# Two-layer diffusion trunk: most adaLN modulations computed on TensorE, and the first feed-forward begun on half of its scale

## The chip, the cores and the metric

The kernel runs on one core of a Trainium2 chip, as one program with one launch. The core has five engines that run side by side, each through its own list of instructions in order: TensorE (PE in the profile; its weight loads are PEld), VectorE (DVE), ScalarE (ACT), GpSimd (POOL) and SyncE (SP), which here starts nearly all the DMAs. The metric is the device time of an execution in microseconds (us).

## The reference, cut to what matters

The program is one step of a two-layer trunk over 128 context and 256 latent tokens of width 1024, in float32. All of a layer that matters here is this:

```python
mod = einsum('bd,de->be', silu(cond), w_ada) + b_ada     # w_ada 1024 x 9216, cond: c_ctx or c
mod = mod.reshape(batch, 9, 1, 1024)
h = rms_norm(x, norm_g[0]) * (1.0 + mod[:, 1]) + mod[:, 0]
x = x + 0.5 * mod[:, 2] * swiglu(h, w_gate[0], w_up[0], w_down[0])     # FFN_DIM = 2816
h = rms_norm(x, norm_g[1]) * (1.0 + mod[:, 4]) + mod[:, 3]
x = x + mod[:, 5] * mix(h)                                             # four mixers
h = rms_norm(x, norm_g[2]) * (1.0 + mod[:, 7]) + mod[:, 6]
x = x + 0.5 * mod[:, 8] * swiglu(h, w_gate[1], w_up[1], w_down[1])

def swiglu(h, w_gate, w_up, w_down):
    return (silu(h @ w_gate) * (h @ w_up)) @ w_down
```

The nine modulations of a layer are two vectors (one for each stream, `c_ctx` and `c`) times a matrix of 1024 x 9216 floats: 37.7 MB a layer, with little arithmetic. They depend on no token, so they may be computed at any time before the place that needs them.

## The kernel before, in words

The residual is kept feature-major, `xT` of [128, 8, 384]: 8 blocks of 128 features, 384 tokens. A product with a weight matrix keeps float32 accuracy by splitting: `split_unit` (lines 164 to 174) makes of a block of weights a rounded part `whi` on ScalarE (L169) and a rest `wlo` on VectorE (L173, sometimes GpSimd); `mm3` (L184 to 188) issues three matmuls per block of 128 x 128 weights: high by high, high by low, low by high. A matmul of 384 tokens is the unit of work on TensorE.

The order is: start (input, first norm), feed-forward (0,0), mixers of layer 0, feed-forward (0,1), feed-forward (1,0), mixers of layer 1, feed-forward (1,1). A feed-forward first makes 22 pairs of gate and up products (tiles `pg` and `pu`, 1056 matmuls), then the down products (`pd`, 528 matmuls). Right behind a norm, the first few products (`hidden`, L194) use the scaled but not yet normed residual `xs`, and the factor 1/rms and the shift come behind the product; two columns beside the 384 tokens carry the shift.

The modulations come in quarters of 256 columns, 72 in all. Five of the first eight are on TensorE (`ada_rows`, L238): the two conditionings are the stationary operand of 128 x 2, the quarter of `w_ada` is streamed, in float32. The other 67 quarters are done by `ada` (L257) without TensorE: VectorE multiplies and adds for one stream (L268, L271), ScalarE multiplies (L269, L274) and GpSimd adds (L275) for the other; VectorE then transposes and sums (L278, L279), and four small matmuls a batch put the result in place (L285). 28 quarters stand beside feed-forward (0,0), 20 beside (0,1), 16 beside (1,0), none beside (1,1): the hook in `ffn_body` issues the next quarter at a lower priority, and a scheduler at build time, which has a cost model of its own, fixes the order of each engine's list.

`start` (L372) takes the order of its parts from a string: the norm's statistics, three quarters of the shift through VectorE, and four quarters of the scale and one of the shift on TensorE. Only when all eight are done does the first feed-forward begin, since the two shift columns are part of its first products. SP has one queue, in order: an issue that waits for a free buffer holds up those behind it.

## Time and profile before

| | |
|---|---|
| Time, median of 3 runs | 2245.91 us (2243.18 to 2248.57) |
| Profiled execution, first to last instruction | 2244.0 us |
| PE busy | 2076.3 us, 93% |
| DVE busy | 1724.6 us, 77% |
| ACT, POOL busy | 1039.3 us, 942.2 us |
| HBM traffic over the span | 143 GB/s |

The profiled execution has no time of its own on the page beside its span; the median of the runs lies 1.9 us above that span, and this is taken as what lies around it. A matmul's busy time in the rows overlaps with the next one's, so rates are read from stretches of known work. Line numbers are those of the kernel before.

### The profile page before, as it was taken

The page shows a single profiled execution, that of the slowest core. Times are in us where ns is not written, and L with a number is a line of the kernel's source. Part 1 is how long each engine was busy: PE and PEld are TensorE (multiplying, and loading weights), DVE is VectorE, ACT ScalarE, POOL GpSimd, SP SyncE. Part 2 cuts the span into 40 slices and gives each one's busy share as a digit, 9 for nine tenths or more (in the row PEclk, how much of TensorE's full clock was granted, in tenths as well). Part 3 has the DMA queues.
Part 4 walks back from the last instruction along what each step waited for, and adds up shares of the span by engine and source line. Part 5 has one row for each costly group of instructions (what it writes and reads, how often), then busy time and mean ns, then how long its engine had stood idle before and what let it go on. Part 6 is the DMA issues. An engine that isn't in the chain of part 4 may idle for free. (4 is left out here: it accounts for less than half of the span.)

```text
span 2244.0 us, 33102 instructions
## 1 busy us (share of the span) xinstructions
PE 2076.3 (93%) x12150; PEld 1992.7 (89%) x12150; DVE 1724.6 (77%) x3198; ACT 1039.3 (46%) x1978; POOL 942.2 (42%) x855
## 2 busy tenths in 40 slices
PE   6988888999789997998998999999987999999999
PEld 3988788999679997998887999998976899999999
DVE  8999998778995469999899974467999745764433
ACT  5666554634234235765556643354333332463322
POOL 5556666433655237366476520134354531500000
PEclk8999999999889999999999999999998999999999
DMA  9466655444333244566555644344442321444342
GB/s 306 152 217 199 202 198 164 129 136 105 83 81 103 60 164 155 169 210 214 186 193 155 206 135 133 128 146 137 119 95 83 109 76 59 160 134 129 115 139 76
DMA packets 316515, 323.08 MB, mean 144 GB/s; under 512 B 42112, under 2 KB 287296, under 8 KB 315840
## 3 DMA queue, kind: packets, MB, share of 16 engines
q1 hardware_dynamic: 316080, 320.70, 46.1%
q8 instruction: 95, 1.56, 0.3%
q14 instruction: 68, 0.56, 0.1%
q10 hardware_dynamic: 272, 0.26, 0.0%
HBM read 313.25 MB, written 7.69 MB: 143 GB/s over the span
## 5 line engine op out<-in xcount | busy, mean ns | idle before, releaser
L169 ACT CAST whi<-raw 128x1024 fp32r<-128x1024 f32 x422 | 440.2, 1045 | 511.1 <-PE mg L187 133.3
L173 DVE TENSOR_TENSOR wlo<-raw,whi 128x1024 fp32r<-128x1024 f32 x324 | 434.8, 1343 | 226.9 <-ACT whi L169 223.8
L275 POOL TENSOR_TENSOR acc<-acc,acct 128x256 f32<-128x256 f32 x469 | 440.5, 939 | 334.7 <-ACT acct L274 306.4
L173 POOL TENSOR_TENSOR wlo<-raw,whi 128x1024 fp32r<-128x1024 f32 x98 | 244.9, 2505 | 289.9 <-ACT whi L169 244.2
L271 DVE SCALAR_TENSOR_TENSOR acc<-araw,cond,acc 128x256 f32<-128x256 f32 x469 | 323.5, 690 | 6.3
L274 ACT ACTIVATE acct<-araw,cond 128x256 f32<-128x256 f32 x469 | 214.1, 501 | 139.7 <-DVE accr L278 83.4
L188 PE MATMUL pd<-hh,wlo 128*128 128x384 f32 x704 | 240.8, 345 | 20.2 <-DVE wlo L173 20.2
L186 PE MATMUL pd<-hh,whi 128*128 128x384 f32 x704 | 240.5, 342 | 9.0 <-ACT whi L169 4.5
L187 PE MATMUL pd<-hl,whi 128*128 128x384 f32 x704 | 239.9, 341 | 0.0
L188 PE MATMUL pg<-hhi,wlo 128*128 128x384 f32 x544 | 184.8, 340 | 19.2 <-DVE wlo L173 19.0
L188 PE MATMUL pu<-hhi,wlo 128*128 128x384 f32 x544 | 184.7, 340 | 13.4 <-DVE wlo L173 13.1
L186 PE MATMUL pg<-hhi,whi 128*128 128x384 f32 x544 | 182.1, 335 | 0.4 <-ACT whi L169 0.4
L187 PE MATMUL pu<-hlo,whi 128*128 128x384 f32 x544 | 182.2, 335 | 0.0
L186 PE MATMUL pu<-hhi,whi 128*128 128x384 f32 x544 | 182.2, 335 | 0.0
L187 PE MATMUL pg<-hlo,whi 128*128 128x384 f32 x544 | 182.1, 335 | 0.0
L186 PE MATMUL mg<-hhi,whi 128*128 128x384 f32 x512 | 177.7, 347 | 0.0
L187 PE MATMUL mg<-hlo,whi 128*128 128x384 f32 x512 | 175.4, 343 | 0.0
L188 PE MATMUL mg<-hhi,wlo 128*128 128x384 f32 x512 | 174.5, 343 | 0.5 <-DVE wlo L173 0.5
L321 POOL TENSOR_SCALAR xg<-xT,gs 128x128 f32<-128x128 f32 (+1 forms) x96 | 101.9, 1074 | 150.9 <-DVE xT L432 150.8
L188 PEld LDWEIGHTS pd<-hh,wlo 128*128 128x128 f32 x704 | 134.0, 191 | 27.6 <-DVE wlo L173 27.6
L186 PEld LDWEIGHTS pd<-hh,whi 128*128 128x128 f32 x704 | 134.4, 191 | 11.3 <-ACT whi L169 5.4
L187 PEld LDWEIGHTS pd<-hl,whi 128*128 128x128 f32 x704 | 134.5, 191 | 0.1
(410 smaller groups left out, 4961.5 us busy)
## 6 DMA issues: line engine op xcount, KB each, us to landing
araw<-in_w_ada SPq DMA_DIRECT2D x67, 1024.0 KB
raw<-in_w_in SPq DMA_DIRECT2D x62, 1024.0 KB
raw<-in_ffn_w_gate SPq DMA_DIRECT2D x44, 1024.0 KB
raw<-in_ffn_w_up SPq DMA_DIRECT2D x44, 1024.0 KB
raw<-in_ffn_w_down SPq DMA_DIRECT2D x40, 1024.0 KB
raw<-in_w_branch SPq DMA_DIRECT2D x16, 512.0 KB
raw<-in_w_out SPq DMA_DIRECT2D x8, 1024.0 KB
raw<-in_w_ada SPq DMA_DIRECT2D x5, 1024.0 KB
```

The costliest lines, as they stand in the source:

```text
L169: nc.scalar.copy(hi, src)
L173: (eng or nc.vector).tensor_tensor(lo, src, hi.bitcast(F32), op=ALU.subtract)
L186: nc.tensor.matmul(ps, w[0], x[0], start=start, stop=False)
L187: nc.tensor.matmul(ps, w[0], x[1], start=False, stop=False)
L188: nc.tensor.matmul(ps, w[1], x[0], start=False, stop=stop)
L271: nc.vector.scalar_tensor_tensor(acc[0], raw[:, kk], self.cond[:, kk:kk + 1], acc[0], op0=ALU.mult, op1=ALU.add)
L274: nc.scalar.mul(t, raw[:, kk], self.cond[:, 8 + kk:9 + kk])
L275: self.last_add = nc.gpsimd.tensor_tensor(acc[1], acc[1], t, op=ALU.add)
L321: self.nc.gpsimd.tensor_scalar(xg[kk][:, a:e], self.xT[:, kk, a:e], gs[:, s, kk:kk + 1], None, op0=ALU.mult)
```

## The change

Of the 72 quarters, 54 go through TensorE as 27 halves of 512 columns, and 18 remain on VectorE, ScalarE and GpSimd. For a half, the two conditionings stand in 32 columns, the rest zeros (`cond32`), and the 8 blocks of `w_ada` go round the four groups of 32 columns of the array (`tile_position=(0, 32 * g)`), so that each group makes a part sum on its own 32 partitions of one PSUM tile: two blocks for each group, 8 matmuls with 512 float32 columns. `issue_after` chains the eight behind each other and behind the last product issued before. ScalarE copies the tile, four transposes turn it, and one VectorE reduction adds the four groups. In the feed-forwards two halves share one PSUM tile (the second writes its own columns of it), one copy and four transposes. There are 9, 6, 6 and 2 such halves in feed-forwards (0,0), (0,1), (1,0) and (1,1), one after every pair of units or so; the 18 quarters stand beside the down products of the first three, six each.

`start` now loads a half of the scale, then the first gate and up weights, then the other half, and begins six units (144 matmuls: gate and up of the first 256 columns, gate of the next) with the first half of the features as soon as that half of the scale is there; the shift comes later. Since the shift is not there yet, its effect on these six units is computed apart, as the same kind of grouped product of the raw weights with the shift (`pair_rows_times`, three times 8 matmuls of 256 columns), and added as a bias. The constants that the start loads shrink from 642 to 162 columns.

```diff
+        cond32 = self.const.tile([128, KD, 34], F32, name="cond32")
+        nc.vector.memset(cond32, 0.0)
+        nc.vector.tensor_copy(cond32[:, :, 2:4], self.cond.rearrange("p (s k) -> p k s", s=2))
+        self.cond32 = [cond32[:, :, 2 - 2 * i:34 - 2 * i] for i in range(2)]
...
+    def ada_load(self, l, mod, hf):
+        c0 = mod * D + 512 * hf
+        raws = []
+        for i in range(2):
+            raws.append(self.ap.tile([128, 4, 512], F32, tag="araw", name="araw", bufs=self.n_araw))
+            self.last_load = self.nc.sync.dma_start(raws[i], self.I["w_ada"][l, 512 * i:512 * i + 512, c0:c0 + 512].rearrange(
+                "(k p) n -> p k n", p=128))
+        return raws
+    def group_rows(self, ps, cols, blocks, first=True, last=True, behind=None):
+        for i, (kk, blk) in enumerate(blocks):
+            g = kk % 4
+            with self.after(behind):
+                behind = self.nc.tensor.matmul(ps[32 * g:32 * g + 32], cols[:, kk], blk, start=(i < 4 and first),
+                                               stop=(i >= 4 and last), tile_position=(0, 32 * g))
+    def group_cols(self, ps, n, e, out):
+        nc = self.nc
+        row = self.ring.tmp([128, n], "mrow")
+        nc.scalar.copy(row, ps)
+        tp = self.mxps([128, n // 128, 128], "acol")
+        for q in range(n // 128):
+            nc.tensor.transpose(tp[:, q], row[:, 128 * q:128 * q + 128], self.k(K_ID))
+        nc.vector.tensor_reduce(out, tp.rearrange("p q (g e) -> p e q g", g=4)[:, 0:e], axis=AX, op=ALU.add)
+    def pair_rows_times(self, cols, blocks, n, out):
+        ps = self.mxps([128, n], "arow")
+        self.group_rows(ps, cols, list(enumerate(blocks)))
+        self.group_cols(ps, n, 2, out)
+    def ada_half(self, l, mod, hf, raws):
+        t = self.small.tile([128, 2, 4], F32, tag="asum", name="asum")
+        self.pair_rows_times(self.cond32[0], [r[:, g] for r in raws for g in range(4)], 512, t)
+        c = slice(8 * mod + 4 * hf, 8 * mod + 4 * hf + 4)
+        self.nc.vector.tensor_tensor(self.mods[l][:, :, c], t,
+                                     self.prm[l][:, R_B:R_B + 72][:, c].unsqueeze(1).to_broadcast([128, 2, 4]), op=ALU.add)
+    def ada(self, *halves):
+        raws = self.ada_load(*halves[0])
+        for i, h in enumerate(halves):
             yield
-    def ada(self, l, mod, n=4):
-        """The same beside the tensor engine, n quarters from a modulation on, one at a time."""
-        nc = self.nc
-        ap = self.ap
-        xa = ap.tile([128, 2, 8 * n], F32, tag="xa", name="xa", bufs=1)
+            if i % 2 == 0:
+                ps, n = self.mxps([128, 512], "arow"), min(2, len(halves) - i)
+            r = i % 2
+            self.group_rows(ps, self.cond32[r], [(4 * h + g, raws[h][:, g]) for h in (1, 0) for g in range(4)],
+                            r == 0, r == n - 1, self.last_mm)
+            if r == n - 1:
+                t = self.small.tile([128, 4, 4], F32, tag="asum", name="asum")
+                self.group_cols(ps, 512, 2 * n, t[:, 0:2 * n])
+                for q, (l, mod, hf) in enumerate(halves[i - r:i + 1]):
+                    c = slice(8 * mod + 4 * hf, 8 * mod + 4 * hf + 4)
+                    self.nc.vector.tensor_tensor(
+                        self.mods[l][:, :, c], t[:, 2 * q:2 * q + 2],
+                        self.prm[l][:, R_B:R_B + 72][:, c].unsqueeze(1).to_broadcast([128, 2, 4]), op=ALU.add)
+            if i + 1 < len(halves):
+                raws = self.ada_load(*halves[i + 1])
...
-        next(shift)
+        wg, wu = I["ffn_w_gate"][0, 0], I["ffn_w_up"][0, 0]
+        def cols(w, c0):
+            t = self.ring.tile([128, KD, 256], F32, name="raw0")
+            nc.sync.dma_start(t, w[:, c0:c0 + 256].rearrange("(k p) n -> p k n", p=128))
+            return t
+        scale = [self.ada_load(0, 1, 0)]
+        raw = [cols(wg, 0), cols(wu, 0)]
+        scale.append(self.ada_load(0, 1, 1))
+        raw.append(self.wcols(wg, 256))
+        shift = [self.ada_load(0, 0, hf) for hf in range(2)]
+        self.up1 = self.wcols(wu, 256)
+        sh32 = self.ring.tile([128, KD, 32], F32, name="sh32")
+        nc.gpsimd.memset(sh32, 0.0)
+        units = [(0, 0), (1, 0), (0, 1), (1, 1), (2, 0), (2, 1)]
+        w, ps = {}, {}
+        def split(u):
+            r, m = u
+            w[u] = self.split_unit(raw[r][:, :, 128 * m:128 * m + 128], [128, KD, 128])
+            ps[u] = (self.mmps if r < 2 else lambda name: self.mxps([128, T], name))(name="pg" if r != 1 else "pu")
+        def rows(u, k0, k1):
+            for k in range(k0, k1):
+                self.mm3(ps[u], (w[u][0][:, k], w[u][1][:, k]), [t[:, k, 0:T] for t in self.xs], k == 0, k == KD - 1)
+        for hf in range(2):
+            self.ada_half(0, 1, hf, scale[hf])
+            self.scales(0, 0, self.nx[2], 4 * hf, 4 * hf + 4)
+            for k in range(4 * hf, 4 * hf + 4):
+                self.early_part(k, True)
+            if hf == 0:
+                for u in units[:3]:
+                    split(u)
+                    rows(u, 0, 4)
+        for u in units[:3]:
+            rows(u, 4, KD)
+        self.rstd()
+        for u in units[3:]:
+            split(u)
+            rows(u, 0, KD)
+        for hf in range(2):
+            self.ada_half(0, 0, hf, shift[hf])
         self.early_shift()
-        with self.after(self.last_add):
-            for k in range(KD):
-                self.norm_scale(k)
+        nc.vector.tensor_copy(sh32[:, :, 0:2], self.mods[0][:, :, 0:8].rearrange("p s k -> p k s"))
+        bias = []
+        for r in range(3):
+            bias.append(self.small.tile([128, 2, 2], F32, tag="sb", name="sb", bufs=3))
+            self.pair_rows_times(sh32, [raw[r][:, kk] for kk in range(KD)], 256, bias[r])
+        self.ready = [(ps[u], bias[u[0]][:, :, u[1]]) for u in units]
+        for k in range(KD):
+            self.norm_scale(k)
         self.norm()
...
+    def ffn_body(self, l, i, jobs, beside, nxt):
         nc, I = self.nc, self.I
         g = None
 
         def hook(n):
-            with self.tc.high_priority(offset=-100):
-                for _ in range(n):
-                    next(jobs, None)
+            for _ in range(n):
+                next(jobs, None)
+        hook(1)
         hh, hl = [], []
         for j in range(KF // 2):
-            rg = self.wcols(I["ffn_w_gate"][l, i], 256 * j)
-            ru = self.wcols(I["ffn_w_up"][l, i], 256 * j)
+            begun = 2 - j if (l, i) == (0, 0) and j < 2 else 0
+            rg = None if begun else self.wcols(I["ffn_w_gate"][l, i], 256 * j)
+            ru = None if begun == 2 else self.up1 if begun else self.wcols(I["ffn_w_up"][l, i], 256 * j)
             for m in range(2):
                 f = 2 * j + m
-                wg = self.split_unit(rg[:, :, 128 * m:128 * m + 128], [128, KD, 128])
-                wu = self.split_unit(ru[:, :, 128 * m:128 * m + 128], [128, KD, 128])
-                pg = self.hidden(wg, "pg")
-                pu = self.hidden(wu, "pu")
+                wg = None if begun else self.split_unit(rg[:, :, 128 * m:128 * m + 128], [128, KD, 128])
+                wu = None if begun == 2 else self.split_unit(ru[:, :, 128 * m:128 * m + 128], [128, KD, 128])
+                pg = self.shifted(*self.ready.pop(0)) if begun else self.hidden(wg, "pg")
+                pu = self.shifted(*self.ready.pop(0)) if begun == 2 else self.hidden(wu, "pu")
                 sg = self.wp.tile([128, T], F32, tag="nt", name="sg", bufs=2)
                 nc.scalar.activation(out=sg, in_=pg, func=AF.Silu)
                 nc.vector.tensor_tensor(sg, sg, pu, op=ALU.mult)
@@ -466,12 +558,11 @@
                 hl.append(self.ring.tile([128, T], F32R, name="hl"))
                 nc.scalar.copy(hh[f], sg)
                 nc.vector.tensor_tensor(hl[f], sg, hh[f].bitcast(F32), op=ALU.subtract)
-            hook(2)
+            hook(1)
         if nxt is None:
             self.nx = None
         else:
             self.norm_begin(*nxt)
-            self.scales(*nxt, self.nx[2])
         g = self.gates(l, 2 * i, 0.5)
         cuts = {(0, 3): (0, 4), (1, 1): (4, 6), (1, 3): (6, 8)}
         for dg in range(2):
...
                         units = []
                 hook(1)
+                if f % 8 == 0:
+                    with self.tc.high_priority(offset=-100):
+                        next(beside, None)
+            if nxt is not None and dg == 0:
+                self.scales(*nxt, self.nx[2])
             for d in range(4):
                 self.down(units, acc[d], d, hh, hl)
                 self.resid(g, 4 * dg + d, acc[d])
                 if nxt is None and (dg, d) in cuts:
                     self.store(*cuts[dg, d])
-        for _ in jobs:
+        for _ in chain(jobs, beside):
...
             self.setup()
+            self.n_araw = 4
             with self.pool("ap") as self.ap:
                 self.start()
+            self.n_araw = 3
             for l in range(2):
                 if l:
                     self.norm()
                 else:
                     with self.after(self.last_load):
                         self.nc.sync.dma_start(self.cst[:, NC1:], self.I["cst2"])
-                self.ffn(l, 0, self.ada(l, 5, 16) if l else chain(self.ada(l, 2, 12), self.ada(l, 5, 16)), (l, 1))
+                halves = {(0, 0): (4, 13), (0, 1): (16, 22), (1, 0): (25, 31), (1, 1): (34, 36)}
+                quarters = {(0, 0): ((0, 6, 2, 2), (0, 7, 0, 4)), (0, 1): ((1, 2, 0, 4), (1, 3, 0, 2)),
+                            (1, 0): ((1, 6, 2, 2), (1, 7, 0, 4)), (1, 1): ()}
+                jobs = [self.ada(*((h // 18, h // 2 % 9, h % 2) for h in range(*halves[l, i]))) for i in range(2)]
+                beside = [chain(*(self.ada_beside(*q) for q in quarters[l, i])) for i in range(2)]
+                self.ffn(l, 0, jobs[0], beside[0], (l, 1))
                 self.norm()
                 self.mixers(l)
                 self.norm()
-                self.ffn(l, 1, iter(()) if l else self.ada(1, 0, 20), None if l else (1, 0))
+                self.ffn(l, 1, jobs[1], beside[1], None if l else (1, 0))
```

The lists of the engines show what this moves. In the rows, the line numbers behind L are those of each kernel's own text (`mm3` is L186 to L188 before, L185 to L187 now). First PE at the start, before: `xr` is the input, `arow` a modulation's row, `mx` from `sqacc` and `nr` the norm, and the last row the first product.

```order
L234 MATMUL mx<-cst,xr 128x128 x24
L246 MATMUL arow<-raw,cond 2x256 x8
L363 MATMUL mx<-cst,sqacc 128x1 x3
L246 MATMUL arow<-raw,cond 2x256 x16
L368 MATMUL mx<-cst,nr 128x128 x3
L251 MATMUL mx<-cst,mrow 128x2 x6
L246 MATMUL arow<-raw,cond 2x256 x16
L251 MATMUL mx<-cst,mrow 128x2 x4
L285 MATMUL mx<-xa,cst 128x12 x4
L186 MATMUL pg<-xs,whi 128x386
```

And now, the same place:

```order
L241 MATMUL mx<-cst,xr 128x128 x24
L261 MATMUL arow<-araw,cond_91 32x512 x8
L271 MATMUL acol<-cst,mrow 128x128 x4
L185 MATMUL pg<-xs,whi 128x384
L186 MATMUL pg<-xs,whi 128x384
L187 MATMUL pg<-xs,wlo 128x384
```

The first product stands behind one half of the scale, where before it stood behind all eight quarters and the norm. Further down PE's list, where the six begun units end, now: `cond_91` is `cond32`, `sh_189` the shift, `raw_169` the raw gate weights.

```order
L187 MATMUL pg<-xs,wlo 128x384
L261 MATMUL arow<-araw,cond_91 32x512 x7
L271 MATMUL acol<-cst,mrow 128x128 x4
L261 MATMUL arow<-araw,cond_91 32x512 x8
L271 MATMUL acol<-cst,mrow 128x128 x4
L185 MATMUL pu<-xs,whi 128x386 x2
L185 MATMUL pg<-xs,whi 128x386
L261 MATMUL arow<-raw_169,sh_189 32x256 x8
L186 MATMUL pu<-xs,whi 128x386
```

The last begun product is followed by both halves of the shift (one of the sixteen matmuls stands further up), each with its four transposes, which wait for ScalarE's copy; the products behind them have 386 columns again, with the shift in them, and the first grouped product for a bias stands between them.

Second, VectorE within the gate and up products of feed-forward (0,0), before: `wlo` is the rest of a weight block, `acc` and `araw` belong to a modulation, `sg` and `hl` to the feed-forward.

```order
L173 TENSOR_TENSOR wlo<-raw,whi 128x1024
L271 SCALAR_TENSOR_TENSOR acc<-araw,cond,acc 128x256 x4
L464 TENSOR_TENSOR sg<-sg,pu 128x384
L271 SCALAR_TENSOR_TENSOR acc<-araw,cond,acc 128x256
L173 TENSOR_TENSOR wlo<-raw,whi 128x1024
L271 SCALAR_TENSOR_TENSOR acc<-araw,cond,acc 128x256
L468 TENSOR_TENSOR hl<-sg,hh 128x384
L278 STREAM_TRANSPOSE accr<-acc 128x256 x2
L268 TENSOR_SCALAR acc<-araw,cond 128x256
L279 TENSOR_REDUCE xa<-accr 128x8 x2
```

And now:

```order
L172 TENSOR_TENSOR wlo<-raw,whi 128x1024
L556 TENSOR_TENSOR sg<-sg,pu 128x384
L172 TENSOR_TENSOR wlo<-raw,whi 128x1024
L560 TENSOR_TENSOR hl<-sg,hh 128x384
L272 TENSOR_REDUCE asum<-acol 128x16
L304 TENSOR_TENSOR mods_87<-asum,vec 128x2x4 x2
```

Seven or eight steps of a modulation stood between one weight block and the next but one; now one reduction and one pair of additions for two halves stand between several weight blocks.

Third, PE where an up unit ends and a gate unit begins, in the same feed-forward, before:

```order
L187 MATMUL pu<-hlo,whi 128x384
L188 MATMUL pu<-hhi,wlo 128x384
L186 MATMUL pg<-hhi,whi 128x384
L187 MATMUL pg<-hlo,whi 128x384
L188 MATMUL pg<-hhi,wlo 128x384
```

And now:

```order
L186 MATMUL pu<-hlo,whi 128x384
L187 MATMUL pu<-hhi,wlo 128x384
L261 MATMUL arow<-araw,cond_91 32x512 x8
L185 MATMUL pg<-hhi,whi 128x384
L186 MATMUL pg<-hlo,whi 128x384
L187 MATMUL pg<-hhi,wlo 128x384
```

Eight grouped matmuls stand unbroken between two units; their transposes come 24 products or more later.

## Rows read from the trace of the kernel before

**Rows 1.** The page, parts 1 and 2: the span, and busy us (share) xinstructions.
```profile
span 2244.0 us, 33102 instructions
...
PE 2076.3 (93%) x12150; PEld 1992.7 (89%) x12150; DVE 1724.6 (77%) x3198; ACT 1039.3 (46%) x1978; POOL 942.2 (42%) x855
```

**Rows 2.** Windows of the feed-forwards: stretch, us, busy us (x) per engine, clock, DMA share, GB/s.
```profile
48.60:264.20 215.60, 195.15 (x1064) 185.79 (x1065) 211.84 (x350) 136.55 (x270) 131.63 (x138) 0.99 0.62 197
264.20:382.50 118.30, 102.60 (x539) 97.23 (x538) 110.19 (x182) 63.48 (x117) 79.61 (x87) 0.94 0.57 182
864.80:1081.00 216.20, 194.50 (x1066) 187.90 (x1065) 211.23 (x348) 135.21 (x265) 122.92 (x128) 0.98 0.58 186
1081.00:1192.40 111.40, 97.80 (x539) 93.58 (x538) 99.10 (x161) 58.81 (x109) 69.55 (x74) 0.98 0.60 196
1192.40:1392.80 200.40, 191.55 (x1075) 187.97 (x1074) 155.82 (x256) 106.87 (x196) 66.78 (x66) 0.98 0.49 153
1392.80:1484.30 91.50, 91.50 (x530) 91.50 (x529) 39.28 (x57) 30.61 (x39) 13.67 (x19) 1.00 0.43 129
1958.20:2144.10 185.90, 185.16 (x1066) 184.80 (x1065) 94.81 (x145) 80.22 (x130) 7.90 (x6) 1.00 0.40 125
```

**Rows 3.** Waits of PE: engine, line, what it waited for: us, times, longest.
```profile
PE pg L188 <- DVE wlo L173: 20.9, 23, 2.1
PE pd L188 <- DVE wlo L173: 20.2, 19, 3.1
PE pu L188 <- DVE wlo L173: 13.5, 16, 1.7
```

**Rows 4.** Groups of instructions by form: busy us, mean ns | idle before.
```profile
L271 DVE SCALAR_TENSOR_TENSOR acc<-araw,cond,acc 128x256 f32<-128x256 f32 x469 | 323.5, 690 | 6.3
...
L278 DVE STREAM_TRANSPOSE accr<-acc 128x256 f32<-128x256 f32 x134 | 52.7, 423 | 8.1 <-POOL acc L275 4.2 <-DVE acc L271 0.5
L279 DVE TENSOR_REDUCE xa<-accr 128x8 f32<-128x256 f32 x134 | 50.7, 406 | 0.1
...
L268 DVE TENSOR_SCALAR acc<-araw,cond 128x256 f32<-128x256 f32 x67 | 23.2, 346 | 2.3 <-DMA araw<-in_w_ada 2.2
...
L314 ACT ACTIVATE sqt<-xT 128x384 f32<-128x384 f32 x42 | 21.5, 518 | 20.2 <-DVE xT L432 17.4 <-DVE sqacc L315 2.7
```

**Rows 5.** Timeline of the start, one row each of DVE, PE, ACT: start us, us, what.
```profile
9.60 2.48 DVE L235 COPY xT<-mx 128x512 f32<-128x512 f32 x4 [0.73 <-PE mx L234]
...
23.24 7.07 PE L246 MATMUL arow<-raw,cond 128*2 128x256 f32 x32
...
37.19 2.87 ACT L345 ACTIVATE xs<-xT,gs 128x128 fp32r<-128x128 f32 x8 [2.82 <-DVE gs L299]
```

**Rows 6.** Timeline of PE in the second mixer stage, at two places.
```profile
1704.31 0.92 PE L1057 MATMUL mx<-bkTs,bqT 32*128 32x384 f32 x6 [0.72 <-DVE bkTs L1044]
1705.16 0.44 PE L188 MATMUL mg<-hhi,wlo 128*128 128x384 f32 x1
...
1764.62 0.55 PE L1074 MATMUL mx<-cst,be 128*128 128x128 f32 x3
1764.92 0.42 PE L188 MATMUL mg<-hhi,wlo 128*128 128x384 f32 x1
```

**Rows 7.** Windows of PE for line 1057 alone: stretch, us, busy us (x), clock, DMA.
```profile
1704.30:1704.40 0.10, 0.09 (x3) 1.00 0.00 0
...
1704.70:1704.80 0.10, 0.10 (x6) 1.00 0.00 0
```

**Rows 8.** Windows of the start, all engines: the DMA in GB/s is last.
```profile
3.00:21.00 18.00, 9.64 (x39) 5.61 (x40) 12.31 (x19) 6.95 (x17) 5.95 (x7) 0.81 1.07 351
```

**Rows 9.** Matmuls of pg and pu to 700 us: duration ns, first and last start us.
```profile
L186 PE MATMUL pg<-xs,whi x40: 332/341/691, 48.6 to 90.4; 128*128 128x386 f32 x40
...
L188 PE MATMUL pu<-xs,wlo x40: 334/340/442, 56.7 to 95.6; 128*128 128x386 f32 x40
```

72 lines of the change are left out of this document (24 added, 48 removed).

## The prediction

> **What bounds the kernel now.** I read the page first: TensorE is busy 93% of the span [rows 1], so time can only come from its waits and from work taken off it, and anything added to it is paid in full unless it fills a wait. Next I cut the trace by windows at the feed-forwards, whose work is the same four times [rows 2]. Feed-forward (1,1), which has no modulations beside it, makes its gate and up products in 185.9 us; the down products of (1,0), by when the modulations are done, take 91.5 us. A clean feed-forward is thus 277.4 us, 0.173 us for each of 528 down matmuls, and TensorE has no gap in it. The others take 215.6 + 118.3 = 333.9 us, 216.2 + 111.4 = 327.6 us and 200.4 + 91.5 = 291.9 us: 56.5, 50.2 and 14.5 us over the clean one, 121.2 us in all. In the four long windows VectorE is busy 89 to 98%, in the clean ones 43 to 51%; and the waits of TensorE that are longest in total in the feed-forwards are for VectorE's `wlo` [rows 3]. So VectorE bounds the first two feed-forwards, and the modulations are what loads it. One quarter costs it 0.346 + 7 x 0.690 + 2 x 0.423 + 2 x 0.406 = 6.8 us [rows 4]. The timeline gave the last part: the first feed-forward product starts at 48.6 us [rows 9], behind all eight quarters of the first norm, while DMA runs at 351 GB/s [rows 8].
>
> **The change part by part.** *Taken from VectorE:* 46 of the 64 quarters that stand in the feed-forwards. At 6.8 us each, 313 us of VectorE's time go; it then has about half its time free in the gate and up products and is no bound there. The 121.2 us shrink to what other causes leave. Part of the 56.5 is the cold beginning of (0,0), and (0,1) and (1,0) begin with the norm's own chain of waits; for these I leave 4 + 3 + 3 = 10 us (bounds 0 and 17).
>
> *Added to TensorE in the feed-forwards:* 23 bursts of eight matmuls. The price of a burst is the main unknown, because the kernel before has no column groups. A float32 product is two records; 32 records of 256 columns take 7.07 us [rows 5], 0.221 us each, so one of 512 columns 0.442. Do groups run side by side? The nearest rows are the attention scores, three float32 products on different groups of 32 rows: their three first records are under way together, the three second ones join 0.4 us later [rows 7], and the next product starts 0.85 us after the first [rows 6]. In series six such records of 384 columns would take 6 x 0.331 = 1.99 us; one product alone is 0.66, so the change of form costs about 0.19 (0.331 is 0.221 x 384/256). If four column groups do likewise, a burst is four records deep: 4 x 0.442 + 0.19 = 1.96 us. Scaled straight from the 0.85 us it is 0.85 / 2 x 512/384 x 4 = 2.27. I take 2.1, between them: 48 us for 23. The far ends are 1.77 (no cost for the form) and 8 x 0.884 + 0.19 = 7.3 (no overlap at all).
>
> The Trainium skill (TensorE: Matmul & The Clock Gate, section "Measured speedup vs the span model") gives 2.38 for three column groups. By that a burst would be about 7.07 / 2.38 = 3.0 us, an estimate, and the sum below some 25 us more; no run here shows it.
>
> *The columns:* 12 pairs or single halves, each one copy on ScalarE, four transposes and a reduction. Three transposes take 0.30 us [rows 6], so four 0.4, and with a change of form 0.5: 6 us (bounds 5 and 12, if the transposes ever wait for the copy; 24 products of 0.17 us stand between). VectorE's reduction and ScalarE's copy lie beside TensorE's work.
>
> *The 18 quarters left* need 18 x 6.8 = 122 us of VectorE, six to a feed-forward, 41 us. In VectorE's new order most of the six of (0,0) stand in the tail of the gate and up products, where it is half free; the down products alone use 43% of it [rows 2]. I take 2 us for each of three feed-forwards, 6 us. At the present price, 121.2 / 64 = 1.9 us a quarter, it would be 34; the lower bound is 0.
>
> *DMA:* the bytes stay, but a half is 2.1 MB in two loads, and SP's list is in order, so a load of `w_ada` that waits for one of three buffers holds the weights behind it. One half and 2.1 MB of weights per 96 products (17 us) need 250 GB/s of the 351 seen [rows 8]; only the first three halves of (0,0) come closer together. I put 3 us (0 to 12).
>
> *The start.* In SP's queue up to the end of the first half of the scale are 0.13 + 0.08 + 1.57 + 2.10 = 3.9 MB, 11.1 us at 351 GB/s [rows 8]; with 1.5 us for the queue to begin (an estimate) they are there at 12.6 us. The four matmuls on its second load come after that, at a clock that may be the lower of the two (0.81 granted on the mean of these us [rows 8]), to some 14.5 us. On ScalarE the row's copy stands behind eight squares that begin when the last input copy ends at 12.1 us: 8 x 0.52, so 16.3 [rows 4, 5]. Copy, transposes, reduction and scales make it 19; four parts of 2.87 / 4 = 0.72 us [rows 5] follow, and the first product stands at about 20 us. The second half of the scale has 8.1 MB before its end, 24.6 us; its parts are done at 32, and the rest of the 144 products, at 0.178 us each, at 46. The shift lands at 47 (15.9 MB), its two bursts and their transposes wait on copies in between, and the next product with a shift begins at 57 us. By then 144 x 0.178 = 25.6 us of work are done, as if the feed-forward had begun at 31.4 instead of 48.6: 17 us less. Three grouped products for the biases take 4 x 0.221 + 0.19 + 0.2 = 1.3 us each, 4 us. Net 13 us saved (bounds 0 and 22; later by 17 us if the first products have to wait for both halves and the shift).
>
> **The sum.** 2244.0 - 13 (start) - 121.2 + 10 + 48 (bursts) + 6 (columns) + 6 (quarters) + 3 (DMA) = 2183 us of span; the median before lies 1.9 above its span, so 2185. By feed-forward: (0,0) and (0,1) gain, (1,0) and (1,1) lose, since they had 14.5 us and nothing to win and get 6 and 2 bursts.
>
> **The rivals.** *Half speed.* The most that a partition feeds TensorE in these rows is 384 elements per 0.173 us; four groups at once, each streaming 512 columns in 0.442 us, want twice that from every partition. Row groups do not: there each partition feeds one product. If that rate is a limit, a burst is 4 x 0.884 + 0.19 = 3.7 us, 1.6 more for 23 bursts and two of the shift, and 2.7 for the biases: +43, 2228. For it: no row shows a faster feed. Against it: nothing.
>
> *In series, the slower side.* If a group's weight load waits for the product of the group before, a burst is 7.3 us: 5.2 more for 25 bursts, 8 us for the biases, 5 for the start: +143, 2328. It decides from a burst of about 4.3 us on: the 61 us gained, over some 28 bursts' worth, are used up at 2.1 + 2.2. Rows 6 and 7 speak against it, but they are row groups. The Trainium skill (TensorE: Matmul & The Clock Gate, section "The mechanism") says that a weight load overlaps matmuls under way only when its row group differs, which column groups never do; by that rule this rival holds, and against it stands the 2.38 that the same page measured. No row here decides it.
>
> *The quarters keep their price.* They stand on VectorE beside `wlo` as before: 34 instead of 6, 2213. For it: VectorE was 93% busy in the down products of (0,0). Against it: six quarters are 41 us, and it has about 50 free in a down stage of its own.
>
> *The start gives nothing* (the change begins early on paper only): if SP's list or the copies hold the first half back until about 37 us, as long as the shift takes, 2198.
>
> **How the numbers follow.** Forecast 0.61, half speed 0.14, series 0.12, quarters 0.08, start 0.05. The likeliest's own range is 2162 to 2212 by its bounds (below: bursts at 1.9 us, the start's best end and no cold beginnings; above: the upper ends of all terms that are no rivals). The range to 2232 takes in quarters, start and most of half speed and leaves out the series. What a measurement can tell from no change is about 0.2%, 4.5 us. Faster: 0.60 of the forecast, 0.12 of half speed, 0.12 of the last two, 0.84. Slower: the series and a little of half speed, 0.13. Same: 0.03.
>
> **What would show it.** Right: the eight grouped matmuls occupy TensorE about 2 us between two ordinary ones; VectorE is about half busy in the gate and up products of (0,0) and (0,1), and both feed-forwards end near 300 us; the waits on `wlo` are gone; the first product starts near 20 us. Wrong: a burst of 4 us or more, bursts that wait for `araw`, products that still wait for `wlo` in the down stage, or a first product after 35 us.

## The result, and the profile after

The changed kernel takes 2195.6 us (median of 4 runs, 2194.7 to 2196.0) where the kernel before takes 2245.2 (4 runs beside it): a ratio of 0.9774, 95% interval 0.976 to 0.9788. The forecast was 2185, with 2162 to 2212 for the likeliest case and 2232 as the upper end of the range: the side and the range held, and the time lies 11 us above. The profiled execution spans 2193.8 us, 50.2 less than before [rows 1]:

```profile
span 2193.8 us, 32394 instructions
...
PE 2090.6 (95%) x12618; PEld 1992.1 (91%) x12618; DVE 1393.2 (64%) x2649; ACT 887.6 (40%) x1604; POOL 613.2 (28%) x513
```

TensorE is busy 14 us more, VectorE 331 us less. The windows that answer to [rows 2]: the down products of (0,0), then gate and up and down products of (0,1), (1,0) and (1,1); columns as there.

```profile
259.10:352.40 93.30, 93.30 (x546) 92.15 (x544) 50.93 (x83) 37.05 (x55) 26.69 (x34) 1.00 0.42 128
...
832.40:1039.00 206.60, 200.34 (x1175) 187.89 (x1174) 136.04 (x223) 101.14 (x179) 45.77 (x46) 1.00 0.57 189
1039.00:1132.50 93.50, 93.50 (x537) 92.27 (x536) 39.10 (x55) 29.15 (x37) 11.66 (x14) 1.00 0.44 148
1132.50:1335.30 202.80, 199.86 (x1183) 188.51 (x1182) 126.06 (x209) 94.54 (x166) 33.99 (x33) 1.00 0.60 197
1335.30:1429.00 93.70, 93.70 (x538) 92.55 (x537) 49.38 (x78) 36.48 (x54) 27.21 (x33) 1.00 0.42 127
...
1904.60:2094.00 189.40, 189.40 (x1102) 185.95 (x1101) 93.79 (x147) 80.06 (x129) 5.77 (x4) 1.00 0.40 129
2094.00:2188.30 94.30, 94.30 (x550) 93.95 (x549) 31.66 (x38) 23.32 (x25) 0.00 (x0) 1.00 0.29 97
```

(0,1) went from 327.6 us to 300.1, (1,0) from 291.9 to 296.5, (1,1) from 280.8 to 283.7. VectorE, 98% busy in the gate and up products of (0,1) before, is 66% busy. Feed-forward (0,0) ends at 352.4 us instead of 382.7 (the last down product starts at 382.3, so it ends just behind the stretch of [rows 2]). The mixers lie between these stretches and take as long as before: 480.0 + 475.6 against 482.1 + 473.8 us. TensorE's waits on `wlo` (line, waited for: us in all, times, longest) answer to [rows 3]:

```profile
PE pg L187 <- DVE wlo L172: 8.4, 6, 2.1
...
PE pu L187 <- DVE wlo L172: 3.6, 4, 1.7
```

They are down to 12.0 us, and none is in the down products, but they are not gone.

A burst in the timeline of TensorE (start, us, what), and its weight loads:

```profile
869.14 0.34 PE L187 MATMUL pu<-xs,wlo 128*128 128x386 f32 x1
869.41 1.92 PE L261 MATMUL arow<-araw,cond 128*32 128x512 f32 x16
871.27 0.44 PE L185 MATMUL pg<-xs,whi 128*128 128x386 f32 x1
871.55 0.34 PE L186 MATMUL pg<-xs,whi 128*128 128x386 f32 x1
```

```profile
869.41 0.16 PEld L261 LDWEIGHTS arow<-araw,cond 128*32 128x32 f32 x8 [0.26 <-issue]
869.87 0.13 PEld L261 LDWEIGHTS arow<-araw,cond 128*32 128x32 f32 x4 [0.30 <-issue]
870.30 0.13 PEld L261 LDWEIGHTS arow<-araw,cond 128*32 128x32 f32 x4 [0.30 <-issue]
```

Products start 0.176 us apart; here 2.41 us lie between 869.14 and 871.55, so the burst costs 2.41 - 2 x 0.176 = 2.06 us. Four loads, one for each column group, and the next four ahead stand in the first row; four more follow 0.46 us later, and four after that: four records deep, as the forecast had it.

The start, in the same view:

```profile
20.00 0.69 PE L185 MATMUL pg<-xs,whi 128*128 128x384 f32 x1 [1.99 <-ACT xs L397]
...
30.11 0.34 PE L187 MATMUL pg<-xs,wlo 128*128 128x384 f32 x1
...
34.61 0.63 PE L185 MATMUL pg<-xs,whi 128*128 128x384 f32 x1 [1.24 <-ACT xs L397]
...
58.33 0.34 PE L187 MATMUL pg<-xs,wlo 128*128 128x384 f32 x1
58.60 1.92 PE L261 MATMUL arow<-araw,cond 128*32 128x512 f32 x14
...
64.43 0.66 PE L271 MATMUL acol<-cst,mrow 128*128 128x128 f32 x4 [0.71 <-ACT mrow L268]
68.76 0.96 PE L185 MATMUL pu<-xs,whi 128*128 128x386 f32 x2 [3.67 <-ACT xs L384]
...
69.98 1.93 PE L261 MATMUL arow<-raw,sh 128*32 128x256 f32 x16
```

The first product stands at 20.0 us, as forecast. By 30.4 the 36 products that the first half of the scale allows are done, and the next one stands at 34.6: between them TensorE has only four grouped matmuls of the second half, its turn, the sums of the norm, and waits. The 144 begun products end at 58.5, not 46, and the first product with shift columns comes at 68.8, not 57, after a wait of 3.67 us. VectorE's timeline shows what the shift's last sums waited for: the turn ends at 65.1, but its reduction (L272) and the addition (L284) stand behind the scaling of the begun products (`hn`) and parts of the norm (`hlo`), which TensorE first reads at 104.8 us.

```profile
65.30 0.55 DVE L210 TENSOR_TENSOR hn<-pg,sqacc 128x384 f32<-128x384 f32 x1
65.76 0.47 DVE L507 SCALAR_TENSOR_TENSOR hlo<-xg,mods,hhi 128x256 fp32r<-128x256 f32 x1
...
66.88 0.18 DVE L272 TENSOR_REDUCE asum<-acol 128x8 f32<-128x32 f32 x1
...
67.85 0.55 DVE L210 TENSOR_TENSOR hn<-pu,sqacc 128x384 f32<-128x384 f32 x1
68.31 0.15 DVE L284 TENSOR_TENSOR mods<-asum,vec 128x8 f32<-128x8 f32 x1
```

### The profile page after: what moved, and what is told of

The parts are those of the page before. It is cut to its first block, busy times and chain, and to the rows that moved or that the text cites. A ratio compares the mean times of both kernels' runs of the same rounds, so it can differ in the third digit from the quotient of the medians.

```text
span 2193.8 us, 32394 instructions
## 1 busy us (share of the span) xinstructions
PE 2090.6 (95%) x12618; PEld 1992.1 (91%) x12618; DVE 1393.2 (64%) x2649; ACT 887.6 (40%) x1604; POOL 613.2 (28%) x513
## 5 line engine op out<-in xcount | busy, mean ns | idle before, releaser
L172 DVE TENSOR_TENSOR wlo<-raw,whi 128x1024 fp32r<-128x1024 f32 x324 | 407.4, 1258 | 376.3 <-ACT whi L168 372.8
L185 PE MATMUL pd<-hh,whi 128*128 128x384 f32 x704 | 238.1, 338 | 0.0
L186 PE MATMUL pd<-hl,whi 128*128 128x384 f32 x704 | 237.7, 338 | 0.0
L326 POOL TENSOR_TENSOR acc<-acc,acct 128x256 f32<-128x256 f32 x126 | 118.7, 942 | 425.8 <-ACT acct L325 417.9
L187 PE MATMUL pd<-hh,wlo 128*128 128x384 f32 x704 | 235.8, 337 | 0.0
L187 PE MATMUL pg<-hhi,wlo 128*128 128x384 f32 x536 | 180.4, 337 | 8.5 <-DVE wlo L172 8.4
L373 POOL TENSOR_SCALAR xg<-xT,gs 128x128 f32<-128x128 f32 (+1 forms) x96 | 92.5, 978 | 332.7 <-DVE xT L523 309.4
L187 PE MATMUL pu<-hhi,wlo 128*128 128x384 f32 x536 | 179.6, 335 | 3.5 <-DVE wlo L172 3.5
L185 PE MATMUL pg<-hhi,whi 128*128 128x384 f32 x536 | 180.6, 337 | 0.0
L186 PE MATMUL pu<-hlo,whi 128*128 128x384 f32 x536 | 179.4, 335 | 0.0
L186 PE MATMUL pg<-hlo,whi 128*128 128x384 f32 x536 | 179.3, 334 | 0.0
L185 PE MATMUL pu<-hhi,whi 128*128 128x384 f32 x536 | 179.1, 334 | 0.0
L185 PE MATMUL mg<-hhi,whi 128*128 128x384 f32 x512 | 177.0, 346 | 0.0
L187 PE MATMUL mg<-hhi,wlo 128*128 128x384 f32 x512 | 174.6, 344 | 0.7 <-DVE wlo L172 0.5
L186 PE MATMUL mg<-hlo,whi 128*128 128x384 f32 x512 | 174.7, 341 | 0.0
L186 PEld LDWEIGHTS pd<-hl,whi 128*128 128x128 f32 x704 | 132.2, 188 | 0.2
L185 PEld LDWEIGHTS pd<-hh,whi 128*128 128x128 f32 x704 | 132.2, 188 | 0.2
L187 PEld LDWEIGHTS pd<-hh,wlo 128*128 128x128 f32 x704 | 132.1, 188 | 0.1
L185 PEld LDWEIGHTS pg<-hhi,whi 128*128 128x128 f32 x536 | 100.6, 188 | 11.7 <-ACT hh L559 9.2
L187 PEld LDWEIGHTS pg<-hhi,wlo 128*128 128x128 f32 x536 | 100.6, 188 | 11.0 <-DVE wlo L172 11.0
```

Of the source, the lines that this page charges most:

```text
L172: (eng or nc.vector).tensor_tensor(lo, src, hi.bitcast(F32), op=ALU.subtract)
L185: nc.tensor.matmul(ps, w[0], x[0], start=start, stop=False)
L186: nc.tensor.matmul(ps, w[0], x[1], start=False, stop=False)
L187: self.last_mm = nc.tensor.matmul(ps, w[1], x[0], start=False, stop=stop)
L326: nc.gpsimd.tensor_tensor(acc[1], acc[1], t, op=ALU.add)
L373: self.nc.gpsimd.tensor_scalar(xg[kk][:, a:e], self.xT[:, kk, a:e], gs[:, s, kk:kk + 1], None, op0=ALU.mult)
```

## The experiments

All are edits of the changed kernel; times are medians of 4 or 5 runs. "End of (0,0)" is the end of the down products of the first feed-forward in the profile, 352.4 us in the changed kernel.

**1. The shift between begun units.** `shift_between`:

```diff
-        for u in units[3:]:
+        for i, u in enumerate(units[3:]):
             split(u)
             rows(u, 0, KD)
-        for hf in range(2):
-            self.ada_half(0, 0, hf, shift[hf])
+            if i < 2:
+                self.ada_half(0, 0, i, shift[i])
         self.early_shift()
```

> The changed kernel with only the place of the shift's two halves moved: between the fourth, fifth and sixth begun unit instead of behind all six. Theory A (the 144 begun products are done at 58.5 us, and behind them a chain of two bursts, copies, turns and the two shift columns keeps TensorE from the next product until 68.8 us; most of that chain can stand beside begun products): of the 10.2 us, the two bursts (2 x 2) stay TensorE's own work and about 6 us of waits go: the first product with shift columns near 63 us, 2189 to 2191 us. Rival B (the shift is late because its loads land late): the same bursts wait for their data at the earlier place, and the time stays at 2194 to 2197.

Measured: 2189.5 us (2186.0 to 2193.1), ratio to before 0.975 (0.9734 to 0.9766). TensorE's timeline:

```profile
42.82 1.06 PE L261 MATMUL arow<-araw,cond 128*32 128x512 f32 x8
...
44.36 1.07 PE L261 MATMUL arow<-araw,cond 128*32 128x512 f32 x8
...
54.09 1.92 PE L261 MATMUL arow<-araw,cond 128*32 128x512 f32 x16
...
62.54 0.62 PE L185 MATMUL pu<-xs,whi 128*128 128x386 f32 x2
```

The first burst of the shift runs in two parts, at 42.8 and 44.4 us, and the second at 54.1, so their data were there 14 and 7.7 us before the changed kernel ran these bursts, at 58.6 and 61.8: rival B falls. The first product with shift columns stands at 62.5, and (0,0) ends at 343.6, 8.8 us earlier; 1.1 of these stood at the first product already (18.9 us instead of 20.0, because the input landed 1.5 us earlier in this execution). Theory A holds. Its time came by a larger gain here and a loss in the layers behind (experiment 6).

**2. The start undone, and the start without begun units.** `old_start` puts back the start of the kernel before (lines 238 to 254 and 372 to 398 there), with three quarters through `ada_beside`. `no_begun` keeps the halves and drops the rest:

```diff
-        scale = [self.ada_load(0, 1, 0)]
-        raw = [cols(wg, 0), cols(wu, 0)]
-        scale.append(self.ada_load(0, 1, 1))
-        raw.append(self.wcols(wg, 256))
+        scale = [self.ada_load(0, 1, hf) for hf in range(2)]
...
-        for u in units[3:]:
-            split(u)
-            rows(u, 0, KD)
```

> The changed kernel with the start of the kernel before: three quarters of the shift through VectorE, five on TensorE with a stationary operand of 128 x 2, no begun units; the feed-forwards stay as changed. Theory A (the new start gains nothing): 2193 to 2199 us, first product at 47 to 49 us, feed-forward (0,0) at its end within 3 us of 352. Rival B (the start is worth the forecast 13 us): 2206 to 2211.

Measured: 2201.9 us (2200.2 to 2203.8), first product at 47.0, end of (0,0) at 354.8. Theory A's places came and the time of neither. In the stretch that the start can touch, the new start is worth 2.4 us; the other 4 us of the difference lie in the layers behind (experiment 6). The forecast's 13 us are not there.

> The changed kernel without begun units: both halves of the scale and both of the shift are loaded first (8 times 1 MB), and the feed-forward begins with all of them, its first ten products with shift columns; no bias products. Theory A (the early beginning gives nothing: only 36 of its products can run before the second half of the scale, and then it waits for the shift): the shift lands after 10.2 MB, some 30 us, the first product with shift stands at 37 to 39 us; the changed kernel has 25.4 us of products done at 68.8 and pays 5.8 us for biases, as if it began at 49. So 8 to 12 us faster than the changed kernel, 2184 to 2188. Rival B (the early products are worth the 13 us that were forecast): 2196 to 2209. Rival C (the loads of w_ada at the head only move the hunger for weights behind them): 2194 to 2198 with waits of TensorE for raw weights after 40 us.

Measured: 2198.2 us (2195.7 to 2198.9), first product with shift at 43.8, end of (0,0) at 347.7. So (0,0) gains 4.7 us, half of what A expected, and the total gains nothing: it lies in rival B's interval and just above C's. For the missing half, the SP list is the likely cause: the issues (start, us, what) put three loads of weights ahead of the shift's, since those wait for the buffers of the scale's halves, and the shift's bursts, from 31.2 to 41.4 us, wait for their loads three times.

```profile
3.05 2.46 SPq L250 DMA_DIRECT2D araw<-in_w_ada  x4
5.55 4.94 SPq L177 DMA_DIRECT2D raw<-in_ffn_w_gate  x1
...
15.84 3.55 SPq L177 DMA_DIRECT2D raw<-in_ffn_w_gate  x1
19.51 7.57 SPq L250 DMA_DIRECT2D araw<-in_w_ada  x4
```

The shift thus had 13.3 MB before its end instead of 10.2, about 9 us more. Rival B, that the early products bring 13 us, falls at the end of (0,0): with them it stands at 352.4, with a plain start at 347.7. The time alone would not decide it. C's waits for raw weights after 40 us are not there.

**3. One column group.** `one_group` (the turn with 32 rows is left out here):

```diff
-            self.group_rows(ps, self.cond32[r], [(4 * h + g, raws[h][:, g]) for h in (1, 0) for g in range(4)],
-                            r == 0, r == n - 1, self.last_mm)
+            behind = self.last_mm
+            for q, (h, g) in enumerate([(h, g) for h in (1, 0) for g in range(4)]):
+                with self.after(behind):
+                    behind = self.nc.tensor.matmul(ps[0:32], self.cond32[r][:, 4 * h + g], raws[h][:, g],
+                             start=(r == 0 and q == 0), stop=(r == n - 1 and q == 7), tile_position=(0, 0))
```

> The changed kernel with the bursts of the feed-forwards in a single column group: all eight matmuls of a half accumulate on the same 32 partitions, and the turn takes 32 rows instead of 128. Theory A (four groups run side by side, so the depth of a burst is two matmuls): in one group a burst is eight deep, 8 x 0.442 + 0.19 = 3.7 us between products instead of 2.1; 23 x 1.65 = 38 us slower, 2230 to 2236. Rival B (a burst costs what its change of form and its loads of weights cost, and groups do not matter): 2193 to 2199. Rival C (a load of weights in the same group waits for the matmul before): 23 x 5.2 = 120 us slower, above 2300.

Measured: 2316.6 us (2311.2 to 2322.2), 121 us slower, 5.3 for each of 23 bursts. TensorE's timeline, then two of the weight loads:

```profile
896.77 7.05 PE L300 MATMUL arow<-araw,cond 128*32 128x512 f32 x16
```

```profile
897.23 0.11 PEld L300 LDWEIGHTS arow<-araw,cond 128*32 128x32 f32 x1 [0.32 <-issue]
897.66 0.11 PEld L300 LDWEIGHTS arow<-araw,cond 128*32 128x32 f32 x1 [0.32 <-issue]
```

My number for theory A was wrong: a float32 product is two records, so eight in a row are 16 x 0.442 + 0.19 = 7.3 us, not 3.7. With that A expects 5.2 us a burst, and that is what came. It cannot be told from C by the time, but by the loads: they follow each other every 0.43 us, the pace of 512 columns alone. A load in the same group costs nothing extra; what four groups save is streaming, 7.05 against 1.92 us, a factor of 3.7.

**4. Bursts broken up.** `singly` issues one grouped matmul behind each product:

```diff
+            if self.pend and next(self.pend[0], self) is self:
+                self.pend.pop(0)
...
+            for h in (1, 0):
+                for g in range(4):
+                    yield
+                    one(ps, r, n, rw[h][:, g], h, g, h == 0)
```

> The changed kernel with the bursts of the feed-forwards broken up: each of a half's eight grouped matmuls stands behind another ordinary product (165 of the 184 stand alone, the rest in one group of three and two of eight). Theory A (a burst is as long as its deepest group, plus a change of form, whether one group works or four): the one matmul that stands alone in the changed kernel's trace, at 49.70 us, puts 1.18 us between two ordinary products, four together put 1.19, eight 2.06. So 165 x 1.18 + 1.2 + 2 x 2.06 = 200 us instead of 23 x 2.06 = 47: 153 us slower, 2340 to 2356. Rival B (a lone one streams 0.88 us and the change of form is hidden): 165 x 0.88 + 5 = 150, 103 us slower, 2293 to 2305. Rival C (it runs beside the products around it): 2193 to 2205.

Measured: 2336.9 us (2336.0 to 2337.4), 141 us slower, just below A's interval and far from B and C. In the timeline one of them between products:

```profile
2054.28 0.33 PE L188 MATMUL pg<-xs,wlo 128*128 128x386 f32 x1
2054.55 1.04 PE L297 MATMUL arow<-araw,cond 128*32 128x512 f32 x2
2055.52 0.45 PE L186 MATMUL pg<-xs,whi 128*128 128x386 f32 x1
2055.81 0.34 PE L187 MATMUL pg<-xs,whi 128*128 128x386 f32 x1
```

From 2054.28 to 2055.81 are 1.53 us, less two products 1.18, as expected. In (1,1), with nothing else beside, two halves cost 204.2 - 185.9 = 18.3 us instead of 3.5. Of the 12 us under A's sum, 10 may be the waits on `wlo`, which shrink where TensorE has more to do: 2.0 us of the 12.0 are left.

**5. What a quarter costs.** Four runs. `no_quarters` makes the 18 quarters nine more halves:

```diff
-                halves = {(0, 0): (4, 13), (0, 1): (16, 22), (1, 0): (25, 31), (1, 1): (34, 36)}
+                halves = {(0, 0): (4, 16), (0, 1): (16, 25), (1, 0): (25, 34), (1, 1): (34, 36)}
```

> The changed kernel with the 18 quarters on TensorE too, as nine more halves: 12, 9, 9 and 2 bursts in the feed-forwards. Theory A (a quarter beside the down products costs 0.3 us, a half on TensorE 2.06 us for its burst and 0.4 us for its share of a copy and four transposes): 5.6 us saved in the down products, 9 x 2.45 = 22 us added, +16, 2209 to 2214; down products at 91.5 us. Rival B (VectorE's load from the quarters also stands behind the waits on wlo, 9.7 us in the gate and up products of the three feed-forwards): up to 10 us less than that, 2199 to 2204. Rival C (a quarter still costs 1.9 us as in the kernel before): 12 us faster, 2181 to 2185.

Measured: 2196.8 us (2195.8 to 2199.0), within 1.3 us of the changed kernel. None of the three numbers came. Windows of (0,1), both stages:

```profile
833.00:1038.50 205.50, 205.50 (x1231) 190.09 (x1231) 96.09 (x161) 82.37 (x133) 5.85 (x4) 1.00 0.62 205
1038.50:1129.90 91.40, 91.40 (x528) 91.40 (x528) 37.99 (x49) 28.87 (x36) 11.29 (x14) 1.00 0.39 126
```

TensorE is never idle there. Nine halves cost 205.5 - 185.9 = 19.6 us, 2.18 each with copies and turns, and 20.1 in (1,0). So 18 quarters cost in the changed kernel what nine halves do here: (0,0) 7.5, (0,1) 300.1 - 296.9 + 3 x 2.2 = 9.8, (1,0) 4.8, together 22 us, 1.2 each. The waits on `wlo` that I had put down to the norm (10 us) went with the quarters: of the 12.0 us, 0.2 are left. `more_quarters` goes the other way:

```diff
+                halves = {(0, 0): range(4, 11), (0, 1): (16, 17, 20, 21), (1, 0): range(25, 29), (1, 1): ()}
...
+            if j in (4, 5, 6, 7):
+                with self.tc.high_priority(offset=-100):
+                    next(beside, None)
```

> The changed kernel with two halves of each feed-forward taken from TensorE and done as four quarters on VectorE, ScalarE and GpSimd, one after each of four pairs of gate and up products (in (1,1) too, which then has no burst): 7, 4, 4 and 0 bursts, 34 quarters. Theory A (VectorE is about a third idle in the gate and up products and takes 27 us more there at the price of the down products, 0.3 us a quarter): 8 x 2.45 = 20 us saved, 5 us added, 2178 to 2184. Rival B (VectorE delays wlo as in the kernel before, 1.9 us a quarter): 30 us added, 2203 to 2208, with waits on wlo of 5 us and more in each feed-forward.

Measured: 2208.4 us (2206.8 to 2214.6), rival B's time, but not its waits: 13.0 us on `wlo` in all, against 12.0. By stretches, two halves fewer and four quarters more cost 3.1 us in (0,0), 1.6 in (0,1), -2.8 in (1,0) and 4.8 in (1,1), and the mixers of layer 1 take 5.6 us longer, with 14 us more of VectorE in them: the list put a part of (1,1)'s quarters there. New are waits of TensorE on other steps of VectorE. One on `hn` is as long as the whole loss in (1,1); the waits on `xT`, 1.7 us in all in the changed kernel, have one of 3.7 us in the mixers of layer 1:

```profile
PE pg L185 <- DVE hn L210: 5.0, 1, 5.0
PE wo L185 <- DVE xT L523: 4.5, 2, 3.7
```

A third of VectorE idle is not room for more quarters. Last, `quarters_down` holds the quarters behind the last gate and up product:

```diff
-                    with self.tc.high_priority(offset=-100):
+                    with self.tc.high_priority(offset=-100), self.after(last_hl):
                         next(beside, None)
```

> The changed kernel with the 18 quarters held behind the last gate and up product of their feed-forward on VectorE's list; in the changed kernel most of them stand among the last gate and up products. The run no_quarters showed what they cost where they stand: without them the nine halves more came to no loss, 2.2 us each, so 18 quarters cost 22 us, 1.2 each, and the waits of TensorE on wlo went with them. Theory A (they cost because wlo of the gate and up products stands behind them; in the down products VectorE has 52 of 91 us free, and six quarters are 41): the waits on wlo go, a down stage costs 2 us more than clean as now, 14 to 16 us faster, 2179 to 2184. Rival B (packed into one down stage they delay its wlo as in the kernel before, where its down stages paid 2.2 to 2.5 us a quarter): 18 x 2.3 = 41 us instead of 22, 2212 to 2218.

Measured: 2197.9 us (2195.8 to 2201.2), neither. Windows of (0,1), and the waits of TensorE in the down products:

```profile
830.40:1028.80 198.40, 198.40 (x1174) 188.11 (x1174) 95.06 (x155) 81.24 (x131) 5.85 (x4) 1.00 0.56 181
1028.80:1129.10 100.30, 95.48 (x538) 93.80 (x536) 81.03 (x123) 49.80 (x84) 52.70 (x56) 0.98 0.52 169
```

```profile
PE pd L187 <- DVE wlo L172: 12.8, 8, 2.8
```

The gate and up stage is 8.2 us shorter and the down stage 6.8 longer. The price moves with the quarter: in the changed kernel all six of (0,1) began among the gate and up products (935.7 to 992.2 us); here they stand among the down products, where VectorE is 81% busy, and in the three feed-forwards together they cost 4 us more, so 1.2 to 1.5 us each wherever they stand.

**6. Combinations, and the mixers.** `both` is more_quarters with shift_between, `down_shift` quarters_down with it, `none_shift` no_quarters with it; they add no edit of their own.

> Four more quarters in each feed-forward (as in the run more_quarters) and the shift's halves between the begun units (as in shift_between). Theory A (the two are independent): the 6 us of the one and the 12 to 17 us of the other add up, 2172 to 2178. Rival B (with the start shorter, the loads of the first bursts and quarters collide with the first weights): 2180 to 2188, with waits of TensorE for raw or araw in feed-forward (0,0).

Measured: 2203.6 us (2199.1 to 2204.1): below more_quarters by 4.8, above the changed kernel, and far above both intervals.

> The quarters in the down products (as in quarters_down) and the shift's halves between the begun units (as in shift_between). Theory A: 6 us below quarters_down, 2173 to 2178. Rival B (quarters cost more in the down products): 2206 to 2212. Rival C (the start's gain is eaten in the mixers by TensorE's clock, as some of it was in shift_between, whose mixers of layer 1 took 5 us longer than those of the changed kernel): the same as quarters_down within 3 us, with feed-forward (0,0) ended 9 us earlier all the same.

Measured: 2194.2 us (2193.0 to 2194.6), 3.6 below quarters_down, with (0,0) ended at 344.6 instead of 354.9 us: nearest to rival C.

> No quarters (as in no_quarters) and the shift's halves between the begun units (as in shift_between). Theory A (independent): 6 us below no_quarters, 2189 to 2192. Rival C (eaten in the mixers by TensorE's clock): 2194 to 2198, with feed-forward (0,0) ended 9 us earlier all the same.

Measured: 2188.8 us (2185.8 to 2192.6), ratio to before 0.9741 (0.9723 to 0.9759), level with shift_between (0.975), and these two are the fastest here: about 7 us better than the changed kernel. That is theory A, 0.2 us past its interval.

A gain at the end of (0,0) did not always arrive: 8.8 us became 6 in shift_between, 4.7 became none in no_begun, 10.3 became 3.6 in down_shift. In the profile of shift_between, which is the slowest of its four runs, it is lost in the mixers of layer 1. Windows of the changed kernel (the whole mixers of layer 1, and two pieces of 30 us), then the same work in shift_between:

```profile
1429.00:1904.60 475.60, 443.69 (x2810) 425.62 (x2810) 360.16 (x782) 186.96 (x381) 209.26 (x153) 0.97 0.38 115
1488.90:1518.90 30.00, 29.12 (x213) 28.13 (x213) 20.59 (x59) 11.58 (x22) 12.59 (x21) 1.00 0.65 195
1608.90:1638.90 30.00, 25.31 (x136) 22.92 (x136) 29.38 (x58) 7.30 (x11) 25.31 (x18) 1.00 0.39 101
```

```profile
1421.50:1902.10 480.60, 450.30 (x2809) 431.75 (x2809) 360.14 (x782) 187.11 (x381) 209.13 (x153) 0.95 0.39 114
1481.20:1511.20 30.00, 27.84 (x181) 26.75 (x180) 16.50 (x50) 10.32 (x20) 10.89 (x20) 0.83 0.53 160
1601.20:1631.20 30.00, 27.15 (x132) 24.40 (x131) 29.11 (x63) 7.64 (x12) 23.38 (x18) 0.83 0.33 83
```

The instructions stand in the same order here. TensorE idles no longer (30.3 us against 31.9), but it is busy 6.6 us more at a lower granted clock: 0.83 in pieces where the other shows 1.00. To see whether this is chance, the changed kernel ran again.

> The changed kernel once more, nothing edited. In the first profile its mixers took 480.2 us (layer 0) and 475.7 us (layer 1); the kernel with the shift between begun units took 481.2 and 480.8, with the same instructions in the same order there, and granted clocks of 0.96 and 0.95 where the first had 0.96 and 0.97. Theory A (TensorE's clock falls behind a wait of the mixers in one execution and not in another): the mixers of layer 1 come out anywhere from 474 to 482 us, with a granted clock that goes with it; time 2193 to 2197. Rival B (it hangs on what stands ahead of them in the program): 480.2 and 475.7 again, within 1 us.

Measured: 2197.3 us (2195.2 to 2199.8); mixers 479.3 and 475.4 us, the second as rival B has it. But two profiles of one kernel do not decide it. The four runs of shift_between took 2186.0, 2187.9, 2191.1 and 2193.1 us at a mean granted clock of 0.983, 0.981, 0.978 and 0.976: the clock differs between executions of one program too. On the other side, all four runs of down_shift lie within 1.6 us, at 0.972 to 0.974. How much of the 5 us belongs to the program, and what decides where the clock falls, stays open.

## Why the prediction was right, and where it failed

| term | forecast, us | measured, us | from |
|---|---|---|---|
| start | -13 | -2.4 | end of (0,0), 354.8 to 352.4 |
| excess of the old feed-forwards | -121.2 | -121.2 | [rows 2] |
| 23 bursts with copies and turns | 48 + 6 | 51 | 23 x 2.2, experiment 5 |
| cold and norm, 18 quarters, DMA | 10 + 6 + 3 | 22 | experiment 5 |
| mixers | 0 | -0.3 | windows |
| sum | -61 | -51 | -50.2 in the spans |

- *What bounds:* right. With most modulations off VectorE, (0,0) ends 30 us earlier and (0,1) takes 27.5 us less, and what VectorE still carries still costs: it is 56 and 66% busy in their gate and up products, where about half was forecast.
- *The burst:* right. 2.06 us against 2.1; the grounds (row groups side by side in [rows 6, 7]) carried over to column groups. Half speed (3.7) and series (7.3) are out; one_group shows what series would have cost, and the 7.3 was its right price.
- The Trainium skill (TensorE: Matmul & The Clock Gate, section "Measured speedup vs the span model") gives 2.38 for three column groups, and the estimate from it was about 3.0 us a burst; four groups measured 3.7 times here, and 2.06 us. A sentence in the section "The mechanism" of the same page of the Trainium skill lets a load overlap only when its row group differs; here loads overlap in other column groups of the same rows (eight loads stand in the first 0.16 us of a burst) and, in one_group, a load in the same group adds no time.
- *The start:* wrong, and this is the 11 us. The step of the prediction that failed: "its parts are done at 32, and the rest of the 144 products, at 0.178 us each, at 46". That took TensorE as busy from 20 us on. But only three units are split by then, with half their features: 36 products, over at 30.4. The other 108 begin at 34.6, the first ten of them 0.32 us apart, the rest 0.176, with one grouped matmul and a few short waits between, and need until 58.5. The 10 us of chain behind them came as forecast (57 - 47; here 68.8 - 58.6), only later, since it stood behind the last of them and not where the shift had landed. By 68.8, 144 x 0.178 = 25.6 us of work were done, as if the feed-forward had begun at 43.2; the three bias products at 1.3 take 4 us, and the clock fell behind the wait:

```profile
68.76:72.00 3.24, 3.24 (x20) 1.52 (x20) 3.24 (x11) 2.25 (x6) 0.00 (x0) 0.51 0.35 130
```

  At 0.51, near the lower of the two levels (1.2 of 2.4 GHz), half of these 3.2 us is lost, so the start stood at 43.2 + 4 + 1.6 = 48.8. Counted alike, the start of the kernel before stood at 52.0 and not at its first product, 48.6 [rows 9]: by 63.95 us it had begun 69 products, 68 x 0.176 = 12.0 us of work. That is some 3 us saved, near the 2.4 of old_start. The first bias burst took 1.93 us here, 1.07 once the clock was back, as in shift_between. With the shift's halves moved, the end of (0,0) is 11.2 us before that of old_start: most of the 13 us were there, one step late.
- *The rival "the start gives nothing", 2198,* was nearly the right time for the wrong reason: the first half was not late; the shift's bursts stood too late in TensorE's list.
- *The quarters:* the sum of the two terms was near (16 against 22), the reasons were not, so this was luck. Nothing is left of a "norm's chain": without quarters the waits on `wlo` vanish. The rival of 1.9 us a quarter was nearer than my 0.33. Part of the 1.2 is not VectorE's: the small matmuls that put a batch in place stand alone among the down products, 0.37 us each, 1.5 us in (0,1). With the 12.0 us of waits on `wlo` these do not fill the 22; the rest is open.
- *DMA:* no burst waits for `araw` outside the start. Right.

## What to carry to other kernels

When work may begin early on part of its input, count how much of it that part allows, and how long the chain is from the last input to the next product: here 36 products, and 10 us of chain that were queued behind everything else instead of between. Grouped matmuls pay when they stand together: a lone one costs 1.18 us, eight 2.06. A "free third" of an engine is no room if an operation that another engine waits for stands in the same list, as `wlo`, `hn` and `xT` do here; price a piece by leaving it out, not by the idle share.

## What was not expected of the hardware

- A lone grouped matmul of 512 columns and four of them in four groups cost the same, 1.18 and 1.19 us between ordinary products.
- The same list of instructions ran 5 us longer in the mixers (475.6 and 480.6 us) in two programs that differ only before, at a granted clock of 0.97 and 0.95. A second profile of the first gave 475.4, yet the four runs of the second program alone lie 7.1 us apart, the slower the lower their mean granted clock (0.983 to 0.976).
- A stretch of 10.2 us with 5.1 us of work for TensorE, ended by a wait of 3.7 us, was followed by 3.2 us at a mean granted clock of 0.51; in shift_between, without that wait, the same work ran at 1.00.
